# Natural token order in the gated branches, split weights kept in DRAM, and the skip term on GpSimd

## The chip, the core and the metric

The kernel runs on one core of a Trainium2 chip. The time is that of one execution on the device in microseconds (us); of several executions the median counts. The engines are PE (matmul), PEld (its weight load), DVE (VectorE), ACT (ScalarE), POOL (GpSimd) and SP (SyncE, which here only issues DMAs); ACT issues DMAs as well, in its own order.

## What is computed

One decoder layer for 2048 tokens of width 1024 in float32. The projection of the normed input feeds three branches and a gate for each of their 1024 output columns:

```
h = rmsnorm(x, g_pre);  proj = h @ w_in              # (2048, 2048)
val, gate = proj[:, :1024], proj[:, 1024:]
y_pool = pool_mixer(val[:, :384], w_pool, pool_scale)       # causal means over 2, 4, 8, 16 tokens
y_ssm  = s5_mixer(val[:, 384:768], ...)                     # diagonal SSM, + d_skip * u, gelu, GLU
y_att  = memory_attention(val[:, 768:], mem, g_mem, w_kv)   # 4 heads over 256 memory tokens
y = concat(y_pool, y_ssm, y_att) * silu(gate)
x = x + rmsnorm(y @ w_out, g_post)
```

## The kernel before

Every large matmul is made of three (`mm3`, L162 to L165): each operand is split into a high part in a reduced float format and a low part, the rest (`split`, L158: ACT copies the high part, DVE or POOL subtracts it for the low part). Tokens come in four chunks of 512; two chunks are a half.

The first stage loads x, forms the SSM inputs, the attention's keys and values, the folded pool weights (stored to DRAM as wpd) and the row norms, which pass through DRAM as rs_b. In the two halves that follow, 13 tasks run in each: two of q, three pairs of a pool branch and its gate, three gates of the SSM part and two of the attention part. Each task multiplies one weight tile of 1024x128 (`w_tile`, loaded raw, then split; high and low part have two buffers each, the raw tile one) with both chunks of the half; `consume` scales the result by the row norm and, in a gate task, forms the gated product yt, which goes to DRAM as yd. The weights are the same in both halves. They are loaded one task ahead (`prefetch`, L1249). Between the tasks the pieces of attention and SSM are woven in; an SSM pair sets up its convolution kernel kst, adds d_skip on its diagonal, and passes it through DRAM (kd, read back as mraw).

yd, the SSM output ysd and the rows of x and out are handled in an order in which the eight tokens of a group lie apart (token = 8j + s, stored as s, j). The last stage reads yd and ysd back, forms the GLU of the SSM branch, splits y, multiplies by w_out and norms.

The instructions of each engine, DMA issues included, run in the order that a scheduler wrote when the program was built; an engine waits for semaphores at the head of its own list. The lines to follow are L160 (low parts: wg_l, wp_l, wq_l of gate, pool and q weights), L159 (high parts), L747 (skip term), L996 and L1001 (yt), L1000 (th), L990, L1030 and L898 (evacuations gp, up, qf), and L116 and L119 (DMA issues of SP and ACT). In the names, a 0 or 1 behind wq, wp or wg is the half.

## Time and profile before

| | us |
|---|---|
| median of 3 runs | 782.86 (781.12 to 782.94) |
| the profiled execution | 782.29 |
| its span in the trace | 780.5 |
| PE, DVE, POOL, ACT busy in it | 719.6, 569.3, 358.9, 344.9 |

All views below come from the profiled execution. Its time is 1.8 us longer than the span, which runs from its first to its last instruction. Busy shares of the whole span mix stages with different limits, so the table by stage is read beside them. PE's busy time counts a matmul to its modelled end, and consecutive matmuls overlap.

### The profile page before, as it was taken

To read this page: it belongs to the slowest core of one execution; us is meant where nothing else is said; L and a number is where in the kernel's file an instruction comes from. 1 tells how busy PE (TensorE), PEld (TensorE's weight loads), DVE (VectorE), ACT (ScalarE), POOL (GpSimd) and SP (SyncE) were. 2 spreads that over 40 slices of the span, in tenths; PEclk is the share of its full clock that TensorE was granted. 3 is DMA by queue.
4 is the path that set the end of the run, shared out by engine and by line. 5 is a ranking of instruction groups with operands and counts; after the bars stand their busy time and mean duration, and the time that the engine had idled before them with its cause. 6 is when DMAs were issued, how large, how long until landed. Compare 5 with 4: busy or idle time off the path is not lost.

```text
span 780.5 us, 10113 instructions
## 1 busy us (share of the span) xinstructions
PE 719.6 (92%) x3449; PEld 582.3 (75%) x3449; DVE 569.3 (73%) x938; ACT 344.9 (44%) x744; POOL 358.9 (46%) x298
## 2 busy tenths in 40 slices
PE   6999769999989899769899869899999999999996
PEld 5788657787778687547687748688888888888885
DVE  4797883899989888997897988877826854244223
ACT  5773512557554634455454534647542414211111
POOL 0059452858678396465737383521132430520221
PEclk9999979999999999999999989999999999999999
DMA  8987943112131325542121212236863646321321
GB/s 264 315 277 235 347 167 104 43 48 83 37 114 42 103 69 156 189 130 76 25 93 42 75 42 75 83 130 195 277 182 112 178 142 189 106 93 45 108 101 62
DMA packets 103347, 100.58 MB, mean 129 GB/s; under 512 B 19184, under 2 KB 80320, under 8 KB 103296
## 3 DMA queue, kind: packets, MB, share of 16 engines
q1 hardware_dynamic: 94144, 83.27, 35.0%
q10 hardware_dynamic: 9152, 16.67, 5.8%
q8 instruction: 27, 0.44, 0.2%
q14 instruction: 24, 0.20, 0.1%
HBM read 74.87 MB, written 25.05 MB: 128 GB/s over the span
## 4 chain that ended last, share of the span: by engine, by line
PE 46%; DVE 27%; DMA 9%; ACT 7%; issue 6%; POOL 3%; ACTq 1%; SPq 0%; DVEq 0%; POOLq 0%
PE pout L165 8%; PE pout L164 8%; PE pout L163 8%; DMA xr<-in_xT_dram 4%; DVE gg L841 3%; DVE yt L1001 3%; PE pjg L163 2%; PE pjg L164 2%; PE pjg L165 2%; DMA rs_x<-in_x_dram 2%; PE pz L163 2%; PE pz L164 2%; PE pz L165 2%; DVE wg_l L160 2%; DVE xl L254 2%
## 5 line engine op out<-in xcount | busy, mean ns | idle before, releaser
L163 PE MATMUL pjg<-xh,wg_h 128*128 128x512 f32 x256 | 103.2, 403 | 1.1 <-DVE gp L990 0.6
L164 PE MATMUL pjg<-xl,wg_h 128*128 128x512 f32 x256 | 102.6, 401 | 0.0
L165 PE MATMUL pjg<-xh,wg_l 128*128 128x512 f32 x256 | 102.3, 399 | 0.0
L164 PE MATMUL pout<-wol,yh 128*128 128x512 f32 (+1 forms) x264 | 102.0, 386 | 0.0
L163 PE MATMUL pout<-woh,yh 128*128 128x512 f32 (+1 forms) x264 | 101.8, 386 | 0.0
L165 PE MATMUL pout<-woh,yl 128*128 128x512 f32 (+1 forms) x264 | 101.7, 387 | 0.0
L1220 POOL TENSOR_TENSOR ov<-ov,xres 128x1024 f32<-128x1024 f32 x15 | 37.0, 2464 | 129.4 <-DVE ov L1219 116.4
L1216 ACT ACTIVATE ov<-pout 128x512 f32<-128x512 f32 x30 | 17.9, 596 | 107.3 <-PE pout L165 88.2
L163 PEld LDWEIGHTS pjg<-xh,wg_h 128*128 128x128 f32 x256 | 48.9, 191 | 13.2 <-DVE gp L990 1.1
L163 PEld LDWEIGHTS pout<-woh,yh 128*128 128x128 f32 x264 | 49.5, 188 | 10.9
L164 PEld LDWEIGHTS pout<-wol,yh 128*128 128x128 f32 x264 | 49.5, 188 | 10.9
L165 PEld LDWEIGHTS pout<-woh,yl 128*128 128x128 f32 x264 | 49.5, 187 | 10.9
L254 DVE SCALAR_TENSOR_TENSOR xl<-xr,gpre,xh 128x512 fp32r<-128x512 f32 x48 | 45.9, 969 | 15.8 <-ACT xh L253 15.6
L165 PEld LDWEIGHTS pjg<-xh,wg_l 128*128 128x128 f32 x256 | 48.7, 190 | 11.3
L164 PEld LDWEIGHTS pjg<-xl,wg_h 128*128 128x128 f32 x256 | 48.8, 191 | 10.5 <-issue 0.4
L838 POOL TENSOR_TENSOR v<-v,ax 128x512 f32<-128x512 f32 x12 | 18.1, 1508 | 76.7 <-DVE ax L837 49.7
L160 POOL TENSOR_TENSOR yl<-yb,yh 128x512 fp32r<-128x512 f32 x20 | 26.6, 1362 | 54.7 <-ACT yh L159 54.7
L1188 DVE SCALAR_TENSOR_TENSOR ow<-ssq,ov 128x1 f32<-128x1 f32 x16 | 6.4, 402 | 58.1 <-ACT ov L1216 58.1
L253 ACT ACTIVATE xh<-xr,gpre 128x512 fp32r<-128x512 f32 x48 | 33.2, 717 | 26.3 <-DMA xr<-in_xT_dram 15.0
L163 PE MATMUL pu<-xh,wsh 128*128 128x512 f32 x96 | 38.8, 419 | 6.2 <-ACT wsh L159 6.0
L164 PE MATMUL pu<-xl,wsh 128*128 128x512 f32 x96 | 38.7, 416 | 0.6 <-DVE xl L254 0.6
L163 PE MATMUL pjp<-xh,wp_h 128*128 128x512 f32 x96 | 38.6, 402 | 0.2 <-DVE gp L990 0.2
(299 smaller groups left out, 1993.6 us busy)
## 6 DMA issues: line engine op xcount, KB each, us to landing
xr<-in_xT_dram SPq DMA_DIRECT2D x32, 256.0 KB
rs_x<-in_x_dram SPq DMA_DIRECT2D x32, 256.0 KB
wg_r<-in_w_in_dram SPq DMA_DIRECT2D x16, 512.0 KB
yd<-yt ACTq DMA_DIRECT2D x16, 512.0 KB
xres<-in_x_dram SPq DMA_DIRECT2D x16, 512.0 KB
out_dram<-ov SPq DMA_DIRECT2D x15, 512.0 KB
yb<-yd SPq DMA_DIRECT2D x40, 128.0 KB
xr<-in_xT_dram SPq DMA_DIRECT2D x8, 512.0 KB
```

The lines of the kernel that those rows point to most:

```text
L160: sub.tensor_tensor(lo, src, hi.bitcast(F32), op=ALU.subtract)
L163: pe.matmul(ps, ahi, bhi, start=first, stop=False)
L164: pe.matmul(ps, ahi, blo, start=False, stop=False)
L165: pe.matmul(ps, alo, bhi, start=False, stop=last)
L253: act.activation(h, xr, AF.Copy, scale=gpre[:, k:k + 1])
L254: dve.scalar_tensor_tensor(l, xr, gpre[:, k:k + 1], h.bitcast(F32), op0=ALU.mult, op1=ALU.subtract)
L838: pool.tensor_tensor(v, v, ax, op=ALU.add)
L841: dve.tensor_tensor_scan(gg[:, i, :], r8[:, g0 + i:g0 + i + 1].broadcast_to([P, NJ]), v[:, i, :], 0.0, op0=ALU.mult, op1=ALU.add,)
L1001: dve.scalar_tensor_tensor(o, branch()[:, cc * CH:(cc + 1) * CH].rearrange(j3, s=T), 0.5, th.rearrange(j3, s=T), op0=ALU.mult, op1=ALU.mult,)
L1188: dve.scalar_tensor_tensor(w, ssq[:, i:i + 1], 1.0 / D, v, op0=ALU.mult, op1=ALU.add)
L1216: act.activation(ov[:, HALVES[n]], ps[n], AF.Square, accum_out=ssq[:, n:n + 1])
L1220: pool.tensor_tensor(ov, ov, xr, op=ALU.add)
```

## The change

Three things are changed.

The gated products are written in the order of the tokens: yt, yd and what reads them have plain rows, one load takes the place of two, and the rows of x and out of a tile are consecutive. Only the SSM output keeps its order in DRAM; it is read in runs of 64 values, and the Gelu on ACT writes it with a stride into token order.

The first half stores the high and low part of each of its 13 weight tiles to DRAM (ws, 512 KB each, issued by ACT); the second half loads them from there straight into the two buffers, without raw tile and split.

The skip term is added by one POOL operation per pair of SSM groups, from a table ddg of diagonal matrices that POOL makes once; before, two DVE operations did it.

```
-    yd = [[dram.tile([P, T, HJ], F32, name=f"yd{i}_{h}") for h in range(2)] for i in range(8)]
+    yd = [[dram.tile([P, SEQ // 2], F32, name=f"yd{i}_{h}") for h in range(2)] for i in range(8)]
...
+        pool.tensor_tensor(
+            ddg,
+            ident[0:GC, 0:GC].unsqueeze(1).broadcast_to([GC, NG, GC]),
+            dsk.unsqueeze(2).broadcast_to([GC, NG, GC]),
+            op=ALU.mult,
+        )
...
-    def w_tile(src, name, raw=None):
+    def w_tile(src, name, raw=None, spill=None, saved=None):
+        wh = wp2.tile([P, KT, P], F32R, tag="whi", name=f"{name}_h")
+        wl = wp2.tile([P, KT, P], F32R, tag="wlo", name=f"{name}_l")
+        if saved is not None:
+            dma(wh.bitcast(F32), saved[0])
+            dma(wl.bitcast(F32), saved[1])
+            return wh, wl
         wr = (raw or wp2).tile([P, KT, P], F32, tag="wraw", name=f"{name}_r", bufs=1)
         dma(wr, src.rearrange("(k p) m -> p k m", p=P))
-        wh = wp2.tile([P, KT, P], F32R, tag="whi", name=f"{name}_h")
-        wl = wp2.tile([P, KT, P], F32R, tag="wlo", name=f"{name}_l")
         split(wh, wl, wr)
+        if spill is not None:
+            dma_later(spill[0], wh.bitcast(F32))
+            dma_later(spill[1], wl.bitcast(F32))
         return wh, wl
...
-        for i in range(2):
-            dve.scalar_tensor_tensor(
-                kst[:, i, P:P + GC],
-                ident[0:GC, 0:GC],
-                dsk[:, g0 + i:g0 + i + 1],
-                kst[:, i, P:P + GC],
-                op0=ALU.mult,
-                op1=ALU.add,
-            )
+        pool.tensor_tensor(kst[:, :, P:P + GC], kst[:, :, P:P + GC], ddg[:, g0:g0 + 2, :], op=ALU.add)
...
-            o = st["y"].rearrange("p s j -> p j s")[:, cc * 64:(cc + 1) * 64, :]
-            j3 = "p (j s) -> p j s"
+            o = st["y"][:, cc * CH:(cc + 1) * CH]
             if branch is None:
-                dve.scalar_tensor_tensor(
-                    o, th.rearrange(j3, s=T), 1.0, gp.rearrange(j3, s=T), op0=ALU.add, op1=ALU.mult
-                )
+                dve.scalar_tensor_tensor(o, th, 1.0, gp, op0=ALU.add, op1=ALU.mult)
...
-            yr = t2k(f"yr{c}_{m}", (P, SPC, NJ))
-            dma(yr, ysd[m * P:(m + 1) * P, ss, :])
+            yr = t2k(f"yr{c}_{m}", (P, T, CJ))
+            dma(yr, ysd[m * P:(m + 1) * P, :, js])
             ge = t2k(f"ge{c}_{m}")
-            act.activation(ge, yr.rearrange("p s j -> p (s j)"), AF.Gelu_apprx_tanh)
+            act.activation(ge.rearrange("p (j s) -> p j s", s=T), yr.rearrange("p s j -> p j s"), AF.Gelu_apprx_tanh)
...
-        t = t2k(f"{name}{c}_{i}", (P, SPC, 2, HJ))
-        for hf in range(2):
-            dma(t[:, :, hf, :], yd[i][hf][:, c * SPC:(c + 1) * SPC, :])
-        return t.rearrange("p s h j -> p (s h j)")
+        t = t2k(f"{name}{c}_{i}")
+        dma(t, yd[i][c // 2][:, (c % 2) * CH:(c % 2 + 1) * CH])
+        return t
...
-        s = c * SPC + tt // 2
-        return s, slice((tt % 2) * P, (tt % 2 + 1) * P)
+        return slice(c * CH + tt * P, c * CH + (tt + 1) * P)
...
-            weights[hf, i] = w_tile(src, f"w{name}")
+            if hf == 0:
+                wsplit[i] = [dram.tile([P, KT, P], F32, name=f"ws{t}{i}") for t in "hl"]
+                weights[hf, i] = w_tile(src, f"w{name}", spill=wsplit[i])
+            else:
+                weights[hf, i] = w_tile(src, f"w{name}", saved=wsplit[i])
```

The scheduler writes each engine's list anew. In brackets stands what an instruction waits for: an engine, or one of the eight counters of the DMAs (DMAHW). The first place is SP's queue early in the second half, before: wp and wg are pool and gate weights (r the raw tile), mraw the SSM kernel, ur the SSM input.

```order
L116 DMA wg_1_r<-in_w_in_dram 128x8x128 [waits DVE_49]
L116 DMA wp_1_r<-wpd 128x8x128 [waits DMAHW5_49,DMAHW1_49,DVE_49]
L116 DMA mraw_3782<-kd_3620 128x1x128 [waits DMAHW2_49,DMAHW6_49,PE_49,Pool_49]
L116 DMA mraw_3782<-kd_3620 128x1x128 [waits DMAHW7_49]
L116 DMA ur_3954<-ud 128x4x64 [waits DMAHW0_49,Pool_49]
L116 DMA ur_3954<-ud 128x4x64
L116 DMA wg_1_r<-in_w_in_dram 128x8x128 [waits DMAHW5_49,DVE_49]
L116 DMA wp_1_r<-wpd 128x8x128 [waits DMAHW6_49,DMAHW2_49,DVE_49]
```

After, in the same place; h and l are the high and low part, wsh and wsl their copies in DRAM:

```order
L116 DMA wp_1_h<-wsh_1487 128x1024 [waits DMAHW4_49,PE_49]
L116 DMA wp_1_l<-wsl_1488 128x1024 [waits PE_49]
L116 DMA wg_1_h<-wsh_1625 128x1024 [waits DMAHW7_49,DMAHW0_49,PE_49]
L116 DMA wg_1_l<-wsl_1626 128x1024 [waits DMAHW2_49,PE_49]
L116 DMA mraw_3822<-kd_3662 128x1x128 [waits DMAHW6_49,DMAHW3_49,Pool_49]
L116 DMA mraw_3822<-kd_3662 128x1x128 [waits DMAHW4_49]
L116 DMA wp_1_h<-wsh_1831 128x1024 [waits DMAHW5_49,PE_49]
L116 DMA wp_1_l<-wsl_1832 128x1024 [waits PE_49]
L116 DMA ur_3991<-ud 128x4x64 [waits DMAHW7_49,DVE_49,Activation_49]
```

A raw tile waited for DVE, which had to have split the one before it; the two reloads wait for PE, which has to be done with the tile whose buffers they take, and the loads of the SSM stand behind them.

The second place is ACT's list in the first half, at the second gate task, before: pex and psc belong to the softmax, gs, mh and lot to SSM and attention.

```order
L159 ACTIVATE wg_0_h<-wg_0_r 128x1024 [waits DMAHW3_49,PE_49]
L829 ACTIVATE gs_1790<-gg_1787 64x512 [waits DVE_49]
L830 ACTIVATE gs_1790<-gg_1787 64x512
L926 ACTIVATE pex_0_0_0_1866,sm_0_0_0_1867<-psc_0_0_0_1850,nb_0_0_0_1864 128x256 [waits DMAHW5_49,DMAHW4_49]
L926 ACTIVATE pex_0_0_0_1866,sm_0_0_0_1867<-psc_0_0_0_1850,nb_0_0_0_1864 128x256
L926 ACTIVATE pex_0_0_1_1876,sm_0_0_1_1877<-psc_0_0_1_1851,nb_0_0_1_1874 128x256 [waits Activation_49]
L926 ACTIVATE pex_0_0_1_1876,sm_0_0_1_1877<-psc_0_0_1_1851,nb_0_0_1_1874 128x256
L992 ACTIVATE th_1_1958<-gp_1_1956 128x512 [waits DVE_49]
L159 ACTIVATE mh_1903<-mraw_1802 128x256 [waits DMAHW7_49,DMAHW6_49]
```

After:

```order
L159 ACTIVATE wg_0_h<-wg_0_r 128x1024 [waits DMAHW3_49,PE_49]
L835 ACTIVATE gs_1806<-gg_1803 64x512 [waits DVE_49]
L836 ACTIVATE gs_1806<-gg_1803 64x512
L119 DMA wsh_2001<-wg_0_h 128x1024 [waits Activation_49]
L932 ACTIVATE pex_0_0_0_1884,sm_0_0_0_1885<-psc_0_0_0_1868,nb_0_0_0_1882 128x256 [waits DMAHW7_49,DMAHW6_49]
L932 ACTIVATE pex_0_0_0_1884,sm_0_0_0_1885<-psc_0_0_0_1868,nb_0_0_0_1882 128x256
L932 ACTIVATE pex_0_0_1_1894,sm_0_0_1_1895<-psc_0_0_1_1869,nb_0_0_1_1892 128x256 x2
L998 ACTIVATE th_1_1978<-gp_1_1976 128x512 [waits DVE_49]
L968 ACTIVATE lot_0_1_1959<-po_0_1_1950 64x256 [waits PE_49,Pool_49]
L119 DMA wsl_2002<-wg_0_l 128x1024 [waits DMAHW4_49,DVE_49]
L159 ACTIVATE mh_1923<-mraw_1818 128x256 [waits DMAHW2_49,DMAHW0_49]
```

The two stores of the split weight have come in, the one of the low part with a wait for DVE, ahead of mh.

The third place is PE at the end of the first stage, before: pf folds the pool weights, rs_t is the transpose of the row norms, pjq the first projection.

```order
L355 MATMUL pf_1236<-wp,wpt_1122 128x96 [waits DMAHW5_49,DVE_49]
L355 MATMUL pf_1236<-wp,wpt_1122 128x96 x3
L355 MATMUL pf_1250<-wp,wpt_1124 128x96 [waits DMAHW2_49,DVE_49]
L355 MATMUL pf_1250<-wp,wpt_1124 128x96 x3
L227 MATMUL rs_t<-ident,rs_y_1282 16x128 [waits DVE_49]
L163 MATMUL pjq_0_0_1374<-xh_0_487,wq_0_h 128x512 [waits DVE_49]
```

After, from the same two folds on:

```order
L356 MATMUL pf_1238<-wp,wpt_1124 128x96 [waits DMAHW3_49,DVE_49]
L356 MATMUL pf_1238<-wp,wpt_1124 128x96 x3
L356 MATMUL pf_1252<-wp,wpt_1126 128x96 [waits DMAHW4_49,DVE_49]
L356 MATMUL pf_1252<-wp,wpt_1126 128x96 x3
L163 MATMUL pjq_0_0_1381<-xh_0_488,wq_0_h 128x512 [waits DVE_49]
L164 MATMUL pjq_0_0_1381<-xl_0_489,wq_0_h 128x512
```

and further on in the same list:

```order
L165 MATMUL pjq_0_1_1412<-xh_4_717,wq_0_l 128x512
L163 MATMUL pjq_0_1_1412<-xh_5_723,wq_0_h 128x512
L164 MATMUL pjq_0_1_1412<-xl_5_724,wq_0_h 128x512
L227 MATMUL rs_t<-ident,rs_y_1284 16x128 [waits DVE_49]
L165 MATMUL pjq_0_1_1412<-xh_5_723,wq_0_l 128x512
L163 MATMUL pjq_0_1_1412<-xh_6_729,wq_0_h 128x512
```

The transpose stood ahead of the first projection; now 41 matmuls of the first two q chunks stand ahead of it. In SP's queue of the same time the load of the first folded pool weights, wp_0_r from wpd, has moved from behind the loads of the row norms rs_b and rs_ct to ahead of them.

## Rows read from the trace of the kernel before

**Rows 1.** Page: busy time of each engine over the span, with its share.
```profile
PE 719.6 (92%) x3449; PEld 582.3 (75%) x3449; DVE 569.3 (73%) x938; ACT 344.9 (44%) x744; POOL 358.9 (46%) x298
```

**Rows 2.** Table by stage: PE PEld DVE ACT POOL busy us (count), PEclk, DMA share, GB/s.
```profile
0.00:113.50 113.50, 96.05 (x457) 78.25 (x457) 90.96 (x196) 61.14 (x116) 50.88 (x58) 0.96 0.83 271
113.50:313.00 199.50, 192.00 (x976) 156.03 (x976) 168.30 (x219) 100.59 (x229) 130.11 (x108) 0.97 0.28 81
313.00:348.00 35.00, 25.20 (x102) 17.90 (x100) 32.78 (x40) 16.91 (x28) 17.70 (x16) 0.95 0.56 178
348.00:545.00 197.00, 178.13 (x908) 144.37 (x909) 165.27 (x212) 101.87 (x232) 98.53 (x85) 0.97 0.27 81
545.00:780.50 235.50, 228.16 (x1010) 185.77 (x1008) 111.98 (x276) 64.35 (x140) 61.68 (x34) 0.99 0.42 134
```

**Rows 3.** Chain of waits from 113.5 to 313, by line, shares of that stretch.
```profile
by line: DVE yt L1001 6.8%; issue 6.3%; DVE gg L841 5.0%; PE pjq L163 4.4%; PE pjq L165 4.1%; PE pjq L164 4.0%; DVE ptl L160 2.9%; POOL s L1040 2.8%; DVE th L1000 2.8%; DVE nb L922 2.7%; PE pjp L164 2.4%; PE pjg L163 2.2%; PE pjg L164 2.2%;
```

**Rows 4.** Chain of waits from 313 to 545: by line; then start, us, what.
```profile
by line: issue 11.0%; PE pjg L163 5.7%; PE pjg L164 5.7%; PE pjg L165 5.6%; DVE wg_l L160 5.4%; DVE gg L841 5.1%; DVE xl L254 3.6%; DVE yt L1001 3.5%; DVE ptl L160 3.4%; DVE nb L922 3.1%; DMA yd<-yt 3.0%; ACT pex L926 2.8%; ACT pex L932 2.8
...
379.98 0.96 ACT wp_h L159
380.96 1.76 DVE wp_l L160
382.72 5.09 issue
...
423.58 1.62 DVE kst L747 x2
...
452.76 1.07 ACT wg_h L159
453.85 8.90 DVE wg_l L160
```

**Rows 5.** Tile yt, pool branches: xcount, duration in ns min/median/max, first and last start.
```profile
L1001 DVE SCALAR_TENSOR_TENSOR yt<-s,th x12: 1072/1350/2103, 171.7 to 482.5; 128x512 f32<-128x512 f32 x12
```

**Rows 6.** Timeline from 448 to 472: start, us, engine line operation [idle before].
```profile
453.85 8.90 DVE L160 TENSOR_TENSOR wg_l<-wg_r,wg_h 128x1024 fp32r<-128x1024 f32 x1 [0.47 <-ACT wg_h L159]
...
459.76 4.75 POOL L1040 TENSOR_TENSOR s<-s 128x1036 f32<-128x1036 f32 x2
...
462.67 2.39 DVE L160 TENSOR_TENSOR hl<-h,hh 128x512 fp32r<-128x512 f32 x1
...
470.11 0.69 DVE L1000 SCALAR_TENSOR_TENSOR th<-th,gp 128x512 f32<-128x512 f32 x1 [0.35 <-ACT th L992]
```

**Rows 7.** DVE's time from 313 to 545 in wg_l, wp_l and wq_l, in this order.
```profile
313.00:545.00 232.00, 17.66 (x8) 0.96 0.31 96
...
313.00:545.00 232.00, 10.24 (x3) 0.96 0.31 96
...
313.00:545.00 232.00, 2.41 (x2) 0.96 0.31 96
```

**Rows 8.** Groups of DVE: line, operation, xcount, busy us, mean ns, idle before.
```profile
L747 DVE SCALAR_TENSOR_TENSOR kst<-ident,dsk,kst 16x16 f32<-16x16 f32 x24 | 11.2, 500 | 0.1
```

**Rows 9.** Timeline of ACT at 389: the store of kst and what follows it.
```profile
389.17 0.33 ACTq L119 DMA_DIRECT2D kd<-kst  x1
389.54 1.09 ACT L159 ACTIVATE pth<-ptp 128x512 fp32r<-128x512 f32 x2 [6.89 <-DVE kst L747]
```

**Rows 10.** Chain of waits from 0 to 113.5, by line.
```profile
by line: DMA xr<-in_xT_dram 26.5%; DMA rs_x<-in_x_dram 15.3%; issue 9.6%; DMA wkv_r<-in_w_kv_dram 5.9%; DVE xl L254 5.2%; DMA wsr<-in_w_in_dram 4.3%; DVE rs_x L195 4.0%; SPq L116 2.8%; DVE wpo L357 2.5%; ACT xh L253 2.4%; ACT rs_x L199 2.2%
```

**Rows 11.** Timeline from 110 to 130: loads of rs_b, first two evacuations of q.
```profile
117.61 0.81 SPq L116 DMA_DIRECT2D rs_b<-rsd  x2
...
121.45 0.69 DVE L898 TENSOR_TENSOR qf<-pjq,rs_b 128x512 f32<-128x512 f32 x1 [7.50 <-PE pjq L165]
...
127.05 0.69 DVE L898 TENSOR_TENSOR qf<-pjq,rs_b 128x512 f32<-128x512 f32 x1 [3.52 <-PE pjq L165]
```

**Rows 12.** What SP waited for: us in total, times, longest us.
```profile
SPq L116 <- DMA wg_r<-in_w_in_dram: 29.5, 10, 3.6
```

More of the change, by code (lines that the diff above doesn't have):

```diff
@@ L275, in hybrid_layer_kernel @@
     halo = tab.tile([P, 3, 15], F32, name="halo")
+    ddg = tab.tile([GC, NG, GC], F32, name="ddg")
     kh = tab.tile([P, 2, NMEM], F32R, name="kh")
@@ L986, in consume @@
             if cc == 0:
-                st["y"] = yp.tile([P, T, HJ], F32, tag="f4k", name=f"yt{i}_{hf}")
+                st["y"] = yp.tile([P, HT], F32, tag="f4k", name=f"yt{i}_{hf}")
             gp = ev(f"gp{i}_{c}")
@@ L1001, in consume @@
                 dve.scalar_tensor_tensor(
-                    o,
-                    branch()[:, cc * CH:(cc + 1) * CH].rearrange(j3, s=T),
-                    0.5,
-                    th.rearrange(j3, s=T),
-                    op0=ALU.mult,
-                    op1=ALU.mult,
+                    o, branch()[:, cc * CH:(cc + 1) * CH], 0.5, th, op0=ALU.mult, op1=ALU.mult
                 )
@@ L1080, in half_tasks @@
         return t
-    SPC = CH // NJ
-    x4 = x.rearrange("(j s) d -> s j d", s=T)
-    o4 = out.rearrange("(j s) d -> s j d", s=T)
+    CJ = CH // T
     woh, wol, glu_st, w3 = {}, {}, {}, {}
@@ L1113, in glu_inputs @@
     def glu_inputs(c):
-        ss = slice(c * SPC, (c + 1) * SPC)
+        js = slice(c * CJ, (c + 1) * CJ)
         gh, gl = ([gx(c, f"g{t}{c}_{m}") for m in range(3)] for t in "hl")
         for m in range(3):
-            yr = t2k(f"yr{c}_{m}", (P, SPC, NJ))
-            dma(yr, ysd[m * P:(m + 1) * P, ss, :])
+            yr = t2k(f"yr{c}_{m}", (P, T, CJ))
+            dma(yr, ysd[m * P:(m + 1) * P, :, js])
             ge = t2k(f"ge{c}_{m}")
-            act.activation(ge, yr.rearrange("p s j -> p (s j)"), AF.Gelu_apprx_tanh)
+            act.activation(ge.rearrange("p (j s) -> p j s", s=T), yr.rearrange("p s j -> p j s"), AF.Gelu_apprx_tanh)
             split(gh[m], gl[m], ge)
@@ L1204, in out_load @@
     def out_load(c, tt):
-        s, js = out_rows(c, tt)
+        rows = out_rows(c, tt)
         xr = w3["op"].tile([P, D], F32, tag="xres", name=f"xres{c}_{tt}")
-        dma(xr, x4[s, js, :])
+        dma(xr, x[rows, :])
         ov = w3["op"].tile([P, D], F32, tag="ov", name=f"ov{c}_{tt}")
@@ L1212, in out_norm @@
     def out_norm(c, tt, ps):
-        s, js = out_rows(c, tt)
+        rows = out_rows(c, tt)
         xr, ov, ssq = out_load(c, tt)
@@ L1220, in out_norm @@
         pool.tensor_tensor(ov, ov, xr, op=ALU.add)
-        dma(o4[s, js, :], ov)
+        dma(out[rows, :], ov)
     def out_last(c, tt):
-        s, js = out_rows(c, tt)
+        rows = out_rows(c, tt)
         xr, ov, ssq = out_load(c, tt)
@@ L1234, in out_last @@
             dve.scalar_tensor_tensor(ov[:, cols], ov[:, cols], r, xr[:, cols], op0=ALU.mult, op1=ALU.add)
-            dma(o4[s, js, cols], ov[:, cols])
+            dma(out[rows, cols], ov[:, cols])
     HALVES = (slice(0, CH), slice(CH, D))
@@ L1246, in hybrid_layer_kernel @@
     first_use = [(hf, i) for hf in range(2) for i in range(NTASK)]
-    weights, tasks = {}, {}
+    weights, tasks, wsplit = {}, {}, {}
     def prefetch(n):
```

## The prediction

> **What bounds the kernel now.** I read the page first: over the whole span PE is busy 92% and DVE 73% [rows 1], which names no limit, since the span has stages with different ones. The table by stage does [rows 2]. In the last stage (545 to 780.5 us) PE works 228.2 of 235.5 us and DVE less than half: PE sets the time there. In the two projection halves (113.5 to 313 and 348 to 545, with the turn between them) DVE is busy 168.3 of 199.5, 32.8 of 35 and 165.3 of 197 us, while PE stands idle for 7.5 + 9.8 + 18.9 = 36.2 us. That idle time counts only whole gaps. So the most that a relief of DVE can give back is near 36 us, and 28.7 us of it lies at the turn and in the second half. The first stage is DMA's: share 0.83 at 271 GB/s.
>
> Then the chain of waits, cut by stage. From 113.5 to 313 the largest single entry is the strided gate product, yt of L1001, with 6.8% of 199.5 us = 13.6 us [rows 3]. From 313 to 545 the split of the gate weights, wg_l, holds 5.4% of 232 us = 12.5 us and yt 3.5% = 8.1 us [rows 4]. So what the change removes is on the chain, but not with all its busy time.
>
> **Gate products in natural order.** The 32 products that write yt with a stride take 1.07 us or more, in the pool branches 1.35 us in the middle [rows 5]. The same kind of operation on the same 128x512 values, contiguous (th<-th,gp), took 0.69 us where nothing disturbed it [rows 6]. I take 1.10 (the quiet ones) against 0.69, 37% less. Beside DVE work this is 32 x 0.41 = 13 us; of the path it is 37% of 13.6 = 5.0 us in the first half and 37% of 8.1 = 3.0 us in the second.
>
> **Weights split once.** In the second half DVE no longer makes the 13 low parts: 17.66 + 10.24 + 2.41 = 30.3 us [rows 7], of which 13 x 1.2 us (the two of wq_l took 2.41 us) is work and the rest stall. ACT loses as many high parts. On the chain stand wg_l with 12.5 us, a wp_l of 1.76 us with an "issue" of 5.09 us behind its start, and three high parts, the first and last of 0.96 and 1.07 us, 3.1 us together [rows 4].
>
> Not all of it comes back. At 453.85 wg_l took 8.90 us. POOL ran additions end to end beside it, the last from 459.76 for 4.75 us, and the next DVE operation, hl, two inputs from SBUF too, then took 2.39 us, against 0.69 us for the quiet th of the same size [rows 6]. If wg_l is gone, hl stands in its place, and 8.9 - 1.2 = 7.7 us of that stall is only handed on. I count 12.5 - 7.7 = 4.8 us. Under the wp_l at 380.96 the next operations read one input from PSUM, so that stall may really go; I count half of its 5.09 us, 2.5. Splits together: 4.8 + 1.8 + 3.1 + 2.5 = 12.2 us. The bounds are 0 (each stall and each copy finds a successor) and 12.5 + 1.8 + 3.1 + 5.1 = 22.5 us.
>
> The Trainium skill says the same more sharply (SBUF — State Buffer, "Who interferes with whom"): a VectorE instruction with two SBUF inputs and a GpSimd instruction that reads SBUF exclude each other for the whole instruction. The 8.90 us row agrees. By that rule the handed-on part is a loss I must not book; without it the splits would give 7.7 us more.
>
> **Skip term.** 24 DVE operations go, 11.2 us in all [rows 8]. One POOL operation on 16x32 values per pair comes, 12 in all; no row has it, the nearest is the pair that it replaces, 2 x 0.5 us, and POOL is busy 98.5 of 197 us in the second half [rows 2, 8], so its work is hidden there. On the chain of the second half I count the one long piece, 1.62 us [rows 4]; in the first half nothing. The wait is the risk: ACT's store of kst waits for it. Now it waits for DVE: after the store at 389.17 ACT's next split had stood 6.89 us [rows 9]. With POOL in DVE's place the wait changes its cause, and I book neither gain nor loss; it could cost or save up to those 7 us once or twice.
>
> **What is added in the first half.** 26 stores of 512 KB, issued by ACT. An issue on that queue takes 0.33 us [rows 9]: 8.6 us on an engine that is busy 100.6 of 199.5 us [rows 2]. The store of the low part waits for DVE's split, and what is queued behind it on ACT (the softmax scaling, mh) waits too; mostly that needs DVE results that come later anyway, as the order shows. I take 1 us, bounds 0 and 8.6.
>
> Four of these stores (2 MB) fall into the first stage, between the splits of the q weights and the loading of x. At the stage's 271 GB/s they are 7.7 us of transfer. DMA's share there is 0.83, so some of it finds room [rows 2], and DMA of xr, rs_x, wkv_r and wsr is 52% of the stage's chain [rows 10]. I take 52% of 7.7 = +4.0 us; bounds 0 and 7.7.
>
> **The start of the projections.** The scheduler now puts 41 projection matmuls ahead of the transpose of rstd on PE, and so into the wait for the norm. But the first q tile leaves its bank only when rs_b has come, at 121.45, 3.8 us after its issue [rows 11]. Two chunk steps at 5.6 us, the distance of the first two q evacuations [rows 11], kept PE busy from 113.5 to 124.7 before. So only about 3.3 us are won. In SP's queue the reload of the folded pool weights now stands ahead of rs_b; it waits for stores that ACT issues before the rstd store, so it should not hold rs_b. Bounds: -3.3 and, were it to hold it for a load of 3 us [rows 12], 0.
>
> **Reloads in the second half.** 13 x 2 copies of 512 KB come from DRAM instead of 13. Each waits on SP for PE to release the slot used two tiles earlier; before, the raw tile was already in SBUF by then. SP stood 29.5 us for ten gate weights to land, 3.0 us each, 3.6 at most [rows 12]. Two copies behind each other: 4 to 6 us after the release, against two chunk steps of 5.6 us and what SSM and attention put between them. It fits, so I count nothing. Its cover is the task in between; if SP is held by an ur or mraw load ahead of it, the cover is gone.
>
> **The last stage.** Half as many yb and sg loads, strided Gelu writes on ACT (64.4 of 235.5 us busy) and rows of x and out in order: all beside a full PE [rows 2]. Zero, from -2 to +3.
>
> **Sum**, against the profiled execution (782.3 us: span 780.5 and 1.8 around it; the median of the runs is 782.9, so nothing is to be shifted): second half -12.2 - 1.6 - 3.0 = -16.8; first half -5.0 + 1.0; start -3.3; first stage +4.0. Together -20.1: 762.2 us.
>
> **Rivals.**
> *DVE is the limit throughout.* Its load falls by 30.3 + 11.2 + 13 = 54.5 us, more than PE's whole idle time. Then all 36.2 us come back: 782.3 - 36.2 + 0.7 (start and first stage) = 747. For it: DVE 94% busy at the turn. Against it: many chain pieces are latencies between ACT, PE and POOL, which stay.
> *Nothing to be seen.* The stalls move to the next operation with two SBUF inputs, the first half is PE's already (192 of 199.5 us), the stores eat the rest: about 781.
> *Late weights: slower.* Place: SP's queue in the second half, where each reload stands behind loads that wait for ACT, DVE or POOL and ahead of the next ones. If each of the 13 tiles is t late, the loss is 13t; it eats the 20.1 us from t = 1.5 us on, and with t = 3.0 us, one landing, the time is 762 + 39 = 801. For it: the raw buffer was a third stage of prefetch, and it is gone. Against it: tasks of 11 us and more between release and need.
>
> **Numbers.** Chances: forecast 0.54, DVE limit 0.20, nothing 0.12, late weights 0.14. The likeliest gives 762; its own range is 748 (splits at their upper bound, first stage at 0) to 778 (splits at 0, first stage at 7.7). For 8 in 10 the range takes in the second case and the third, and leaves out the fourth: 740 to 784. A change under 0.3% (2.4 us) can't be told from none. Faster: 0.54 + 0.20 + 0.05 of the third case = 0.79; same 0.07; slower 0.14.
>
> **What would show it.** In the profile after: yt at about 0.7 us; no wg_l, wp_l, wq_l after 320 us; PE idle of the second half down from 18.9 to near 5 us; the second half's length down by 15 to 20 us, the first's by about 4; the rstd transpose a few us later than 113.1. I am wrong if PE waits there for DMA of the reloaded weights, if DVE's other two-input operations grow by what the splits lose, or if the first stage grows by more than 8 us.

## The result, and the profile after

The changed kernel takes 769.87 us (median of 4 runs, 769.00 to 770.79) against 782.9 us before: ratio 0.9838, 95% interval 0.982 to 0.9857. It is faster by 13.0 us; forecast were 762.0 us in a range from 740 to 784. The profiled execution took 770.79 us with a span of 769.0 us, 11.5 us less than the span before. All comparisons by stage below are of one profiled execution of each kernel. Two kernels whose instructions stand in the same order (the changed kernel and j_gelu) differ by 3.2 us in the first half, so a single stage is read to about 3 us. One run of j_gelu, 866.75 us at a granted clock of 0.75 where its other runs have 0.97, was in a slower state and is left out of its time.

The page of the changed kernel, busy time of each engine with its share of the span, answers to [rows 1]:

```profile
PE 715.6 (93%) x3449; PEld 582.5 (76%) x3449; DVE 538.1 (70%) x901; ACT 338.9 (44%) x731; POOL 354.1 (46%) x311
```

DVE has lost 31.2 us of busy time and 37 instructions; the forecast counted 54.5 us of relief. Much of the rest has come back in hl, the low part of the SSM state: from the 24th evacuation to the end of the second half it takes 29.1 us, against 12.0 us before. The table by stage, cut at the corresponding places (columns as in [rows 2]):

```profile
0.00:113.50 113.50, 98.93 (x473) 82.39 (x474) 88.94 (x188) 60.69 (x117) 53.19 (x59) 0.94 0.91 296
113.50:313.00 199.50, 186.22 (x962) 152.02 (x960) 161.44 (x215) 100.20 (x227) 126.95 (x116) 0.97 0.40 133
313.00:346.00 33.00, 25.98 (x102) 19.13 (x100) 28.46 (x35) 15.02 (x26) 16.75 (x16) 0.90 0.65 220
346.00:532.00 186.00, 176.38 (x909) 143.60 (x910) 145.20 (x189) 91.80 (x217) 92.84 (x88) 0.97 0.36 117
532.00:769.00 237.00, 228.08 (x1008) 185.39 (x1007) 114.08 (x277) 71.20 (x145) 64.34 (x35) 1.00 0.41 135
```

The reader is to see two things. In the second half (346 to 532) PE's idle time is 9.6 us instead of 18.9, so the gain lies there. In the first half (113.5 to 313) DVE is relieved by 7 us and PE nevertheless stands idle for 13.3 us instead of 7.5. Of the difference, 3.8 us lie ahead of the second evacuation of q (126.9), which comes no later than before.

The tile yt, which answers to [rows 5] (engine line, operation, xcount, duration in ns min/median/max):

```profile
L1004 DVE SCALAR_TENSOR_TENSOR yt<-s,th x12: 680/1167/1816, 178.9 to 472.3; 128x512 f32<-128x512 f32 x12
L1001 DVE SCALAR_TENSOR_TENSOR yt<-th,gp x12: 680/692/1765, 257.5 to 509.7; 128x512 f32<-128x512 f32 x12
L1004 DVE SCALAR_TENSOR_TENSOR yt<-attn,th x8: 684/692/1548, 303.3 to 535.0; 128x512 f32<-128x512 f32 x8
```

The contiguous product has the predicted 0.69 us in two of its three places. In the pool branches the median is still 1.17 us. The sum of the 32 fell from 44.6 to 32.3 us.

The chain of waits from 313 to 532, by line, answers to [rows 4]:

```profile
by line: DVE hl L160 12.1%; DMA xr<-in_xT_dram 6.3%; issue 6.2%; PE pjg L163 6.0%; PE pjg L165 6.0%; PE pjg L164 6.0%; DVE gg L847 5.2%; ACT pex L932 4.3%; ACT pex L938 3.8%; DVE ptl L160 3.8%; DVE xl L254 3.7%; DVE nb L928 2.5%; DVE ml L16
```

wg_l is gone, and hl, which was not among the largest entries before, holds 12.1% of 219 us = 26.5 us. What this means is seen in the timeline around 412, which answers to [rows 6] (start, us, engine, line, operation, idle before in brackets):

```profile
412.44 1.27 POOL L818 TENSOR_TENSOR cc<-cc,tq 128x512 f32<-128x512 f32 x1
...
412.62 8.64 DVE L160 TENSOR_TENSOR hl<-h,hh 128x512 fp32r<-128x512 f32 x1
...
413.67 1.26 POOL L787 TENSOR_TENSOR ur<-ur,rs_ct 128x512 f32<-128x512 f32 x1
...
414.90 1.91 POOL L1038 TENSOR_TENSOR s<-up 128x1038 f32<-128x1038 f32 x1
...
416.77 1.27 POOL L822 TENSOR_TENSOR ss<-ss,tr 128x512 f32<-128x512 f32 x1
...
418.01 0.64 POOL L728 TENSOR_TENSOR rt<-Bre,XT__113 128x256 f32<-128x256 f32 x1
...
418.59 0.24 POOL L760 TENSOR_TENSOR kst<-kst,ddg 16x32 f32<-16x32 f32 x1
...
418.80 1.90 POOL L1038 TENSOR_TENSOR s<-s 128x1036 f32<-128x1036 f32 x1
...
421.31 0.38 PE L164 MATMUL py<-hl,oh 128*128 128x256 f32 x1 [3.00 <-DVE hl L160]
```

One DVE subtraction that elsewhere takes 0.69 us (at 507.15, for one) stands for 8.64 us, as long as POOL runs seven operations end to end; it ends 0.6 us after the last of them. PE waits 3.00 us for it. At 447.75 hl takes 9.06 us in the same way.

### The profile page after: what moved, and what is told of

It is laid out like the page before. It is cut to its first block, busy times and chain, and to the rows that moved or that the text cites. A ratio compares the mean times of both kernels' runs of the same rounds, so it can differ in the third digit from the quotient of the medians.

```text
span 769.0 us, 10087 instructions
## 1 busy us (share of the span) xinstructions
PE 715.6 (93%) x3449; PEld 582.5 (76%) x3449; DVE 538.1 (70%) x901; ACT 338.9 (44%) x731; POOL 354.1 (46%) x311
## 4 chain that ended last, share of the span: by engine, by line
PE 43%; DVE 23%; ACT 5%; issue 3%; DMA 2%; POOL 1%; ACTq 0%; DVEq 0%; SPq 0%; POOLq 0%
PE pout L165 8%; PE pout L164 8%; PE pout L163 8%; DVE hl L160 4%; PE pjg L163 3%; PE pjg L164 3%; PE pjg L165 3%; DVE gg L847 3%; PE pz L163 2%; PE pz L165 2%; PE pz L164 2%; DMA xr<-in_xT_dram 2%; DVE ptl L160 2%; ACT pex L932 1%; DVE yt L1004 1%
## 5 line engine op out<-in xcount | busy, mean ns | idle before, releaser
L254 DVE SCALAR_TENSOR_TENSOR xl<-xr,gpre,xh 128x512 fp32r<-128x512 f32 x48 | 43.9, 924 | 18.1 <-ACT xh L253 18.0
L164 PEld LDWEIGHTS pjg<-xl,wg_h 128*128 128x128 f32 x256 | 48.7, 190 | 10.1
L844 POOL TENSOR_TENSOR v<-v,ax 128x512 f32<-128x512 f32 x12 | 16.5, 1373 | 74.1 <-DVE ax L843 64.1
L932 ACT ACTIVATE pex<-psc,nb 128x256 f32<-128x256 f32 x64 | 29.5, 474 | 28.0 <-DVE nb L928 27.5
L1182 DVE SCALAR_TENSOR_TENSOR ow<-ssq,ov 128x1 f32<-128x1 f32 x16 | 2.7, 168 | 55.1 <-ACT ov L1210 55.0
```

What stands on the lines that cost most here:

```text
L164: pe.matmul(ps, ahi, blo, start=False, stop=False)
L254: dve.scalar_tensor_tensor(l, xr, gpre[:, k:k + 1], h.bitcast(F32), op0=ALU.mult, op1=ALU.subtract)
L844: pool.tensor_tensor(v, v, ax, op=ALU.add)
L932: act.activation(pex[:, s, :], psc[o][:, s, :], AF.Exp, bias=nb[:, s:s + 1], accum_out=sm[:, s:s + 1],)
```

## The experiments

Each edit makes the scheduler write all lists anew, so most kernels differ in more than their edit; the text says where that matters. Three pairs that differ by the natural order alone keep the order of their compute instructions up to 6 us ahead of the first pz: before and a_order, g_splits_sp and m_splits_order_sp, h_splits_skip and the changed kernel. The table has the kernels in the order of the text: median time; start of the second evacuation of q; from there to the 24th evacuation (the last but two of the first half), called first half; from there to the first pz, called second half although it has the turn in it; and from pz to the last instruction of PE, DVE or ACT, called last stage. All are read from timelines of DVE and PE.

| kernel | us | start | first half | second half | last |
|---|---|---|---|---|---|
| before | 782.9 | 127.0 | 180.8 | 237.4 | 232.2 |
| changed (all three) | 769.9 | 126.9 | 180.5 | 224.4 | 234.2 |
| a_order | 776.9 | 127.2 | 177.2 | 233.3 | 234.2 |
| b_splits | 767.5 | 126.9 | 186.0 | 218.1 | 232.2 |
| c_skip | 775.0 | 125.3 | 180.0 | 231.8 | 232.2 |
| d_order_skip | 771.9 | 129.5 | 175.9 | 227.2 | 234.2 |
| g_splits_sp | 762.2 | 124.6 | 180.5 | 220.8 | 232.2 |
| k_all_sp | 763.4 | 125.8 | 175.3 | 223.0 | 234.2 |
| h_splits_skip | 775.0 | 126.7 | 186.0 | 226.2 | 232.2 |
| m_splits_order_sp | 759.8 | 125.0 | 177.3 | 218.5 | 234.2 |
| f_noq | 768.9 | 127.9 | 178.0 | 223.1 | 234.2 |
| j_gelu | 769.7 | 125.8 | 183.7 | 222.5 | 234.2 |
| n_hl_pool | 775.4 | 123.8 | 177.7 | 230.0 | 236.9 |
| p_small_pool | 741.8 | 124.8 | 171.0 | 206.9 | 234.2 |

**Each edit alone.** The first four take the three edits apart.

a_order: the kernel before with the changes of yt, yd, the last stage's loads and rows.

> The kernel before with the natural token order alone; weights split anew in the second half, skip term on DVE. Theory 1 (the parts act where they stood on the chain; the first half has no slack that DVE's relief could give back): yt falls to about 0.69 us, the first half stays within 1 us of the kernel before, the second half wins at most 3.0 us; time 779 to 783. Rival 2 (the order wins about 4 us in the first half, as predicted, and the 26 stores of the changed kernel ate it): first half 4 us shorter, time about 775. Rival 3 (any DVE time removed counts alike: 13.0 us won for 31 us of DVE busy time gone, so 0.42 us per us): 13 us of DVE time gone give about 5 us, time 777.

Measured: 776.87 us, ratio 0.9923 (0.9907 to 0.9939). The first half is 3.6 us shorter, the second 4.0, the last stage 2.0 longer. Theory 1 falls: the first half does have slack that a relief of DVE gives back, and the terms of the forecast (5.0 and 3.0 us) were about right for this edit. The two other pairs that differ by the natural order alone give 3.2 and 5.5 us in the first half, 2.3 and 1.8 us in the second.

b_splits: the kernel before with the changes of w_tile and prefetch.

> The kernel before with the stored split weights alone; strided yt and DVE skip term as before. Theory 1: nearly the whole gain of the second half (14.6 us) is here, so 10 to 13 us in the second half; the first stage costs about what the changed kernel shows (rstd transpose near 119 us); time 769 to 774. Rival 2 (stores eat 4 us in the first half): the first half 4 us LONGER than before, time about 774 to 778. Rival 3 (0.42 us per us of DVE time): 13 low parts of 1.2 us, 15.6 us, plus the stall with them, give 7 to 12 us, time 771 to 776.

Measured: 767.5 us, ratio 0.9808 (0.9788 to 0.9828): this one edit alone wins 15.4 us, more than all three together. The second half is 19.3 us shorter, more than any of the theories gave, and the first half 5.2 us longer, as rival 2 said.

c_skip:

```
-        for i in range(2):
-            dve.scalar_tensor_tensor(
...
+        pool.tensor_tensor(kst[:, :, P:P + GC], kst[:, :, P:P + GC], ddg[:, g0:g0 + 2, :], op=ALU.add)
```

> The kernel before with the skip term by one POOL operation per pair alone. Theory 1: 1.6 us in the second half, nothing in the first: time 780 to 783, same as before within what can be told. Rival 3 (0.42 us per us of DVE time): 11.2 us gone give 4.7 us, time 778. Rival 4 (the new wait of ACT's store for POOL costs up to 7 us once or twice): slower, 785 to 795.

Measured: 774.95 us, ratio 0.9899 (0.9883 to 0.9916). It wins 8.0 us, more than any theory gave: 1.7 us at the start, 0.8 in the first half, 5.6 in the second. All lists are others here, and what of the gain is the edit's own is not shown.

d_order_skip: in the changed kernel, both halves call `w_tile(src, f"w{name}")`.

> The changed kernel without the stored weights: natural order and POOL skip term, but each half loads and splits its weights as before. Theory 1: the sum of the two alone, at most 4.6 us, and the first half as long as in both kernels within 1 us; rstd transpose back near 113 us; time 778 to 782. Rival 2 (the stores ate the first half's gain): the first half 4 us shorter than in both kernels, time about 774. Rival 3 (0.42 us per us of DVE time): 24 us gone give 10 us, time 773.

Measured: 771.93 us, ratio 0.9863 (0.9845 to 0.9882). The first half is 4.9 us shorter than before, as rival 2 said; the total is near rival 3's. Theory 1 falls here too.

So the edits are worth 6.0, 15.4 and 8.0 us alone, 29.4 us in all, and 13.0 us together. In the first half they add: -3.6 + 5.2 - 0.8 gives +0.8, measured -0.3. In the second half they don't: -4.0 - 19.3 - 5.6 gives -28.9, measured -13.0.

**The stores of the first half.** g_splits_sp is b_splits with the stores issued by SP:

```
-            dma_later(spill[0], wh.bitcast(F32))
-            dma_later(spill[1], wl.bitcast(F32))
+            dma(spill[0], wh.bitcast(F32))
+            dma(spill[1], wl.bitcast(F32))
```

> Stored split weights alone, but the 26 stores of the first half are issued by SP and not by ACT. With ACT's stores the first half (second q evacuation to the last gate evacuation) took 186.0 us against 180.8 before, and ACT stood at the head of its list for about 6.7 us there until DVE had made a low part. Theory 1 (that wait on ACT is the price): the first half comes back to 181 to 182 us, the second half keeps its gain, time about 763. Rival 2 (the price is the other order of work on DVE, attn behind wg_l and ahead of PE's psc): first half stays near 186 us, time 766 to 769. Rival 3 (SP now holds the loads behind the stores, and PE waits for raw weights): first half 190 us or more, time 772 or more.

Measured: 762.17 us, ratio 0.9737 (0.9718 to 0.9755). The first half is back at 180.5 us. Theory 1 holds in place and size. k_all_sp makes the same edit in the changed kernel.

> The changed kernel with its 26 stores issued by SP and not by ACT. Theory 1 (ACT's wait for the low parts costs the first half about 5 us, whatever else is changed): first half (second q evacuation to last gate evacuation) from 180.5 to 175 or 176 us, the rest as in the changed kernel, time 764 to 766. Rival 2 (natural order and skip term had taken that wait away already): first half 179 to 181 us, time 769 to 770.

Measured: 763.44 us, ratio 0.9737 (0.9706 to 0.9768), the first half 175.3 us. Theory 1 again, with a total slightly below its 764 us. What the store does on ACT is to be seen in ACT's timeline of the changed kernel (answering to [rows 9]; ACTq is its DMA issues):

```profile
153.50 1.09 ACT L159 ACTIVATE pth<-ptp 128x512 fp32r<-128x512 f32 x2 [0.21 <-PE ptp L949]
158.66 0.40 ACTq L119 DMA_DIRECT2D wsl<-wp_l  x1
159.09 0.58 ACTq L119 DMA_DIRECT2D kd<-kst  x1
159.72 0.63 ACT L159 ACTIVATE qh<-qf 128x512 fp32r<-128x512 f32 x1 [5.13 <-DVE ptl L160]
```

And DVE's at the same time:

```profile
149.27 6.73 DVE L160 TENSOR_TENSOR ml<-mraw,mh 128x256 fp32r<-128x256 f32 x1 [1.44 <-ACT mh L159]
...
157.40 1.23 DVE L160 TENSOR_TENSOR wp_l<-wp_r,wp_h 128x1024 fp32r<-128x1024 f32 x1
```

wp_l ends at 158.63, and the store of it at 158.66 ends a stand of 4.07 us on ACT (the last pth ended at 154.59). Such stands ahead of the low parts' stores add up to 8.7 us in the first half of the changed kernel and 5.6 us in that of b_splits. ACT has nothing more to do with these stores than to issue them, but what is queued behind them waits for DVE. On SP, a store at 159.28 of k_all_sp waits for wp_l too, with only loads behind it. One caution: with SP's stores the scheduler also writes the first half in an order nearer to that of before (in g_splits_sp, evacuations 2 to 24 lie 2.0 to 2.7 us ahead of before, nearly all at a constant distance). The loss doesn't follow the length of the stands either: 8.7 and 5.6 us of stands go with about the same loss, and f_noq below, whose stands add up to 1.8 us, has a first half of 178.0 us. How much of the 5 us is ACT's stand and how much the order that ACT's stores bring, these runs don't separate.

**The skip term beside stored splits.** h_splits_skip is b_splits with the edit of c_skip.

> Stored split weights and the skip term on POOL, without the natural order. Theory 1 (the edits relieve the same waits of the second half, so they don't add there: splits and all three give 218.1 and 224.4 us for turn and second half): only what the skip term won at the start, about 1.7 us, and in the first half, 0.8 us, is added; time 764 to 767. Rival 2 (they add: 15.4 + 8.0 us): 759 to 760. Rival 3 (the changed kernel's turn, 6 us longer than with splits alone, comes from the skip term on POOL): 769 to 771.

Measured: 774.95 us, ratio 0.9891 (0.9867 to 0.9914), 7.5 us slower than b_splits. Theories 1 and 2 fall; rival 3 has the direction and part of the size. The second half is 8.2 us longer than in b_splits. So the edit that wins 8.0 us in the kernel before costs 7.5 us where the splits are stored. h_splits_skip shows hl at 8.65 and 9.02 us, like the changed kernel. In b_splits another operation stands instead:

```profile
411.85 10.44 DVE L160 TENSOR_TENSOR ml<-mraw,mh 128x256 fp32r<-128x256 f32 x1
```

That exchange is not the main price, as the second half shows when it is cut at the 34th evacuation (columns as in [rows 2]). The changed kernel:

```profile
307.40:396.50 89.10, 78.89 (x369) 61.49 (x368) 72.31 (x91) 42.55 (x96) 51.43 (x47) 0.92 0.41 133
396.50:531.80 135.30, 128.87 (x667) 105.47 (x666) 106.95 (x138) 66.85 (x152) 63.76 (x60) 0.99 0.39 128
```

and b_splits:

```profile
312.90:395.60 82.70, 74.96 (x369) 58.84 (x368) 71.67 (x94) 40.18 (x90) 53.42 (x43) 0.96 0.47 152
395.60:530.90 135.30, 127.53 (x663) 104.80 (x662) 112.63 (x150) 70.16 (x163) 66.58 (x60) 0.97 0.39 127
```

The whole 6.4 us lie in the first part; from the 34th evacuation on the two kernels take the same time. There the two longest hl and the long ml stand: PE waits 6.4 us for hl in the changed kernel, and in b_splits 6.5 us for attn, which stands behind ml, and 0.8 us for hl. The other kernels with stored splits agree: with the skip term on POOL the two parts take 89.2 and 137.0 us (h_splits_skip) and 87.7 and 135.3 us (k_all_sp), with the skip term on DVE 84.1 and 136.7 us (g_splits_sp) and 83.4 and 135.1 us (m_splits_order_sp). In the first part PE's list differs. In the changed kernel a chunk of q stands ahead of an SSM pair's matmuls (pr, pk, py) and waits for the evacuation of q:

```profile
347.92 0.80 PE L163 MATMUL pjq<-xh,wq_h 128*128 128x512 f32 x1 [2.32 <-DVE qf L904]
```

h_splits_skip and k_all_sp have the same wait (2.32 and 2.02 us). In b_splits, g_splits_sp and m_splits_order_sp the SSM pair stands there, and PE has no such wait. In this part the changed kernel's PE is idle for 10.2 us against 7.7 in b_splits (for hl 2.5 against 1.4 us), and its granted clock is 0.92 against 0.96. At these clocks 0.08 x 89.1 against 0.04 x 82.7 us is lost, an estimate of 3.8 us more. So what the skip term costs beside stored splits goes with an order of PE's list that comes with it, and only some 1 us with hl. No run changes that order alone, so its part is argued, not shown.

m_splits_order_sp leaves the skip term on DVE, with the natural order and SP's stores.

> Stored split weights and natural order, stores issued by SP, skip term on DVE as before. Stored splits with SP's stores alone: 762.2 us. Theory 1 (with the splits gone, the skip term on POOL is what costs the second half, since hl there takes 8.6 and 9.0 us beside POOL's additions): turn and second half 216 to 221 us as with the splits alone, first half 176 to 177 us, last stage 234.2 us; time 759 to 762. Rival 2 (the natural order takes the second half's gain): turn and second half 224 us, time 766 or more.

Measured: 759.84 us, ratio 0.9689 (0.9659 to 0.972): theory 1, within 0.3 us of each of its numbers for the stages, though the table above speaks against its reason, the long hl. It is the fastest kernel here that computes all of the reference, 10.0 us ahead of the changed kernel. Against k_all_sp, which has the skip term on POOL, the gain is 3.6 us, with intervals that overlap.

**The stores of the first stage.** f_noq is the changed kernel in which the two q tiles are not stored:

```
-            if hf == 0:
+            if i < 2:
+                weights[hf, i] = w_tile(src, f"w{name}")
+            elif hf == 0:
```

> The changed kernel without the stores of the two q tiles in the first stage; the second half loads and splits these two again. Theory 1 (the 2 MB delay the norm by 6 us, but the projection matmuls put ahead of it fill that time, so they cost nothing): rstd transpose back at 113 to 115 us, second q evacuation still at 127 us, and two low parts more at the turn: time 770 to 772. Rival 2 (as predicted, the stores cost about 4 us at the end): second q evacuation about 3 to 4 us earlier, time 766 to 768.

Measured: 768.89 us, ratio 0.9821 (0.9804 to 0.9838). The transpose of rstd starts at 114.51 us instead of 119.17 us, and the second evacuation of q at 127.9 instead of 126.9 us. So the norm's delay costs nothing where the projection matmuls stand ahead of it: theory 1. In f_noq they don't, its first projection stands behind the transpose as in the kernel before; the run therefore shows stores and early matmuls together, not each alone. The total is below its 770 us; the difference, 2.5 us in the first half, is within what one execution differs from another.

**The last stage.** j_gelu is the changed kernel with this edit:

```
-            act.activation(ge.rearrange("p (j s) -> p j s", s=T), yr.rearrange("p s j -> p j s"), AF.Gelu_apprx_tanh)
+            act.activation(ge, yr.rearrange("p s j -> p (s j)"), AF.Gelu_apprx_tanh)
```

> The changed kernel with the Gelu of the last stage writing contiguously, so the SSM output is not brought into token order there (this part of the result is left out of order). The last stage took 234.2 us in the three kernels with natural order and 232.2 us in the three without; the one PE gap there, 1.65 us, is a pz waiting for DVE's ov. Theory 1 (the strided Gelu, 1.13 us against 0.63 us on ACT, delays the GLU of the next chunk and so the order on DVE): last stage 232.2 us, time about 768. Rival 2 (the rows of x and out, or the loads, are the cause): 234.2 us, time about 770.

Measured: 769.67 us, ratio 0.983 (0.9808 to 0.9853). As the edit shows, the stride is on the side that the Gelu reads (yr, in steps of 64 values); ge is written in order. The Gelu falls from 1129 to 622 ns, and the last stage stays at 234.2 us with its PE gap:

```profile
583.38 0.50 PE L163 MATMUL pz<-gh,wgh 128*128 128x512 f32 x1 [1.65 <-DVE ov L1213]
```

Theory 1 falls by the stage; the time alone would not tell 768 from 770 us. In the last stage of b_splits PE waits for nothing, so the gap is most of the 2.0 us. The instructions of the two kernels stand in the same order, so what is left is that order (a pz whose bank DVE's ov has yet to empty) or the rows and loads; which of them was not tried.

**POOL and the low parts.** Two runs test whether hl is long because POOL works beside it. n_hl_pool moves it:

```
-        split(hh, hl, h)
+        split(hh, hl, h, sub=pool)
```

> The changed kernel with the low part hl of the 12 SSM pairs made by POOL and not by DVE. In the second half of the changed kernel hl held DVE 29.1 us in all (8.64 and 9.06 us in two of six pairs) while POOL ran seven additions end to end, and PE's py waited for it 7.7 us there. Theory 1 (hl only stands in the place of the split that was removed, kept waiting by POOL): POOL's list puts hl ahead of the last additions, so these waits shrink to 3 us or less, DVE's busy time falls by some 30 us, turn and second half from 224.4 to about 217 to 221 us; time 763 to 767. Rival 2 (PE waits for the SSM chain in any case, and DVE's long hl costs nothing): 769 to 771. Rival 3 (the stall goes on to DVE's next operation with two SBUF inputs): hl gone, but ml, rl or yt longer by as much; 769 to 771.

Measured: 775.36 us, ratio 0.9891 (0.9865 to 0.9918), slower than the changed kernel. hl takes 1.3 us on POOL, PE no longer waits for it, and the stall has gone on, as rival 3 said. DVE's timeline of n_hl_pool:

```profile
379.99 9.77 DVE L160 TENSOR_TENSOR ml<-mraw,mh 128x256 fp32r<-128x256 f32 x1
...
390.45 0.43 DVE L969 TENSOR_TENSOR attn<-po,lot 64x256 f32<-64x256 f32 x1
```

and PE's, right behind:

```profile
391.02 0.55 PE L920 MATMUL psc<-kh,qh 64*128 64x256 f32 x1 [4.63 <-DVE attn L969]
```

At the start of the last stage PE then waits 9.61 us for gh, which no theory had foreseen, and the last stage is 2.7 us longer. That is what makes this kernel the slower one: from the 24th to the 52nd and last evacuation it takes 220.4 us against 224.7 in the changed kernel.

p_small_pool makes POOL's work smaller instead:

```
+        pool.tensor_tensor(cc[:, :, 0:16], cc[:, :, 0:16], tq[:, :, 0:16], op=ALU.subtract)
...
+        pool.tensor_tensor(ss[:, :, 0:16], ss[:, :, 0:16], tr[:, :, 0:16], op=ALU.add)
...
+        pool.tensor_tensor(ur[:, :, 0:16], ur[:, :, 0:16], rs_ct[:, 0:16].unsqueeze(1).broadcast_to([P, 2, 16]), op=ALU.mult)
```

> The changed kernel with three of POOL's additions per SSM pair (cc, ss and ur) done on 32 of their 512 columns only, so the rotation tables and the scaled input are left incomplete. In the changed kernel each of the three takes about 1.27 us, and they are three of the seven operations that POOL runs beside the 8.64 us of hl at 412.62. Theory 1 (DVE's long operations wait for POOL's run of additions): the two long hl shrink from 8.6 and 9.1 us to 6 us or less, hl in all from 29.1 to 20 us or less, PE's wait for hl in the second half from 7.7 to 4 us or less, turn and second half from 224.4 to 217 to 221 us; time 763 to 767. Rival 2 (the stall has another cause, the same whatever POOL does): hl stays at 27 to 31 us, time 768 to 771. Rival 3 (the stall shrinks but moves on to another operation that PE waits for): hl shorter, another two-input operation longer by as much, time 768 to 775.

Measured: 741.76 us, ratio 0.9462 (0.9439 to 0.9486), 28.1 us below the changed kernel. The page of this kernel:

```profile
PE 704.6 (95%) x3449; PEld 575.5 (78%) x3449; DVE 508.1 (69%) x901; ACT 338.0 (46%) x731; POOL 319.4 (43%) x311
```

Its stages, first half, turn and second half (columns as in [rows 2]):

```profile
124.80:295.80 171.00, 168.75 (x893) 138.63 (x893) 142.25 (x198) 94.21 (x216) 102.97 (x108) 0.98 0.43 144
295.80:342.20 46.40, 40.49 (x177) 31.09 (x176) 38.32 (x49) 19.79 (x36) 24.86 (x27) 0.93 0.55 185
342.20:502.70 160.50, 160.50 (x862) 132.67 (x862) 121.46 (x179) 88.81 (x212) 72.86 (x80) 1.00 0.40 128
```

And hl in its turn and second half (xcount, busy us, mean ns):

```profile
L160 DVE TENSOR_TENSOR hl<-h,hh 128x512 fp32r<-128x512 f32 x7 | 10.0, 1435 | 0.7 <-ACT hh L159 0.7
```

against the changed kernel's:

```profile
L160 DVE TENSOR_TENSOR hl<-h,hh 128x512 fp32r<-128x512 f32 x7 | 29.1, 4160 | 0.8 <-ACT hh L159 0.8
```

DVE does the same 901 instructions on the same sizes as in the changed kernel and is busy 30.0 us less, with 34.7 us less work on POOL. In the second half proper PE has no idle time left (160.50 of 160.50 us), at a granted clock of 1.00; over the whole kernel it is busy 11.0 us less with the same 3449 matmuls. Theory 1 has the mechanism: with less work on POOL the long hl are gone (2.66 us at most), and no DVE operation takes 4 us any more. The gain is at least four times the 3 to 7 us that it gave, and not all of it is shown to be the stall's. The lists are others here too: up to the 34th evacuation the second half gains 10.1 us, but PE's list there has the SSM pair ahead of the q chunk as in b_splits, and against b_splits it gains 3.7 us; from there to the first pz it gains 7.5 us against either. The edit also shortens POOL's own steps of the SSM chain, which no run separates from the stall. The first half is 9.5 us shorter as well.

The stall as a whole can be counted: for each DVE operation, its duration less the shortest of the same name and shape in the same kernel, summed over the second half (with the turn), in us.

| kernel | all DVE operations | in wg_l, wp_l, wq_l | in hl | in ml |
|---|---|---|---|---|
| before | 56.6 | 14.7 | 7.3 | 4.0 |
| c_skip | 55.4 | 9.8 | 12.7 | 3.0 |
| b_splits | 52.3 | 0 | 5.7 | 14.4 |
| h_splits_skip | 55.6 | 0 | 24.3 | 4.4 |
| changed (all three) | 54.8 | 0 | 24.4 | 4.5 |
| n_hl_pool | 48.2 | 0 | 0 | 13.7 |
| p_small_pool | 33.6 | 0 | 5.3 | 5.7 |

What was taken from one operation others got, within 8.4 us (the seven kernels not listed have 50.0 to 55.2 us); only less work on POOL made the sum fall clearly. In the first half it fell by 8.6 us too (42.3 to 33.7 us). The sum is not a price: b_splits has 4.3 us less of it than the kernel before and a second half 19.3 us shorter. It matters who waits for the operation that is held. The Trainium skill (SBUF — State Buffer, "Who interferes with whom") says that a VectorE instruction with two SBUF inputs and a GpSimd instruction that reads SBUF exclude each other for the whole instruction. The trace agrees, and shows more: the 8.64 us of hl are seven POOL operations in a row, not one.

## Why the prediction was right, point by point, and where it was not

The verdict, the place and the range were right: faster, by the second half, within 740 to 784 us. The time was 7.9 us too low. By its own terms, against the profiled executions:

- **Start and first stage** (-3.3 and +4.0, together +0.7): measured -0.2 at the second evacuation of q. The norm came 6.1 us later, as "a few us" allowed, and cost nothing: without the q stores (f_noq) the start is no earlier. The sum of the two was right; the sizes of the two terms were not measured apart, since f_noq lacks the early matmuls as well as the stores.
- **First half** (-5.0 + 1.0): measured -0.3. The gain from yt was sized about right (3.6 us, a_order). The step that failed is "I take 1 us" for the stores that ACT issues: with the order they bring they cost 5.2 us in b_splits (186.0 against 180.8 us before), 5.2 us in the changed kernel (180.5 against 175.3 us with SP's stores). The bound of 8.6 us held them. I had seen that ACT waits for the low part, and argued that what is behind it needs DVE anyway; the row at 158.66 shows qh behind it for 5.13 us.
- **Splits in the second half** (-12.2, bounds 0 and 22.5): alone they gave -19.3, near the upper bound. The step "7.7 us of that stall is only handed on" was right in kind: the stall of the low parts (14.7 us in wg_l and wp_l) reappears in ml or hl nearly whole. But what it costs depends on who waits for its new carrier: in the second half before, PE waited 13.0 us for hl; in b_splits it waits 6.5 us for attn behind ml and 2.1 us for hl. One reading of the working was off: the "issue" of 5.09 us behind wp_l was wp_l's own, which took 6.92 us at 380.96. That stall did not go either; in the changed kernel hl took 4.68 us at 381.73.
- **Skip term** (-1.6): alone -5.6 in the second half and -8.0 in all; beside the stored splits +8.2 in the second half. The step that failed is to price the edit by the one piece on the chain that it removes, with "its work is hidden there": POOL's added work is small (12 operations, 4.3 us in all), but the lists that come with it are others. Beside stored splits PE's list has the q chunk of 347.92 ahead of an SSM pair, and all of the 6.4 us by which the changed kernel's second half is longer than that of b_splits lie ahead of the 34th evacuation, where that chunk stands. The two longest hl, which came with the edit, stand where no time is lost against b_splits.
- **yt in the second half** (-3.0): alone -4.0. On top of stored splits it gives -2.3 (m_splits_order_sp against g_splits_sp) and -1.8 (changed against h_splits_skip), less than a single stage can be read to.
- **Reloads** (0): right. PE has no wait for a weight's DMA in the second half; SP waited for PE to release the slots, as said. What SP waited for in the changed kernel (us in total, times, longest), answering to [rows 12]:

```profile
SPq L116 <- PE pjg L165: 82.7, 6, 20.6
...
SPq L116 <- DMA wg_r<-in_w_in_dram: 10.0, 2, 5.1
```

- **Last stage** (0, from -2 to +3): measured +2.0, in each of the kernels with natural order but n_hl_pool, where it is 4.7. It was inside the bounds. The strided Gelu is not the cause; most of it is one wait of PE, 1.65 us.

The stages as measured: -0.2 - 0.3 - 13.0 + 2.0 = -11.5 us, as the spans differ. The second half came near its term (-16.8) by errors that cancel: the splits gave 7.1 us more than counted, and the three edits together 6.4 us less than the splits alone. One sign of being wrong came true: DVE's other two-input operations grew by what the splits lost (hl's excess from 7.3 to 24.4 us, against 14.7 us of stall in the splits), and the kernel was faster all the same. So of the rivals, "nothing to be seen" had its mechanism right and its price wrong; late weights did not occur; and "DVE is the limit throughout" was nearer to the truth than its chance said, in another form: DVE is kept waiting by POOL, and the three edits together took 1.8 us from that excess.

Open is why the scheduler writes the q chunk ahead of the SSM pair in one case and behind it in the other, and likewise sets hl or ml beside POOL's run; how the 5 us of ACT's stores divide between the stand and the order; and how much of p_small_pool's gain is the stall.

## What to carry to other kernels

Where DVE's operations show three or ten times their shortest duration, count that excess over the stage before pricing an edit: here removing the operation that carried it moved it to another one, and only less work on the engine beside it (POOL) made it fall. Then look at who waits for the operation that will be held. A store that is issued from a compute engine's queue waits there for its data and holds what is queued behind it; here issuing 26 stores from SP, which has only transfers, won 5.3 and 6.4 us. Where a scheduler writes the lists, cut the stage finely and find where the time is lost before naming the longest operation as the cause: here it was not. Edits that each win alone are to be measured together: here 29.4 us became 13.0, and leaving one out and moving the stores (m_splits_order_sp) made it 23.7 (783.51 to 759.84 us).
